# A hybrid DeltaNet and windowed-attention layer on one core: the first head's inverse gets its pool beside that head's tiles and stands ahead of the projections' close, and the ordering plan prices transfers by packets

## The chip, the cores and the metric

The kernel runs on one core of a Trainium2 chip. A core has five instruction streams: PE (TensorE, matrix products), DVE (VectorE), ACT (ScalarE), POOL (GpSimd) and SP (SyncE, which here issues every transfer); 16 DMA engines move the data between HBM and the on-chip memories SBUF and PSUM. Every stream runs its instructions in the order in which they were built. The metric is the device time of one execution in microseconds (us).

## The reference

One layer over 2048 positions of width 1024, all in float32. After a row norm, one projection feeds two groups of heads:

```python
h = rms_norm(x, norm_w[l])
proj = h @ w_in[l]
dn_q, dn_k, dn_v, dn_z, dn_beta, dn_decay, sw_q, sw_k, sw_v, sw_z = split(proj, cuts)
dn = gated_deltanet_bidir(dn_q, dn_k, dn_v, dn_beta, dn_decay, ...)
dn = rms_norm(dn, dn_out_norm_w[l]) * silu(dn_z)
sw = windowed_gqa_with_sinks(sw_q, sw_k, sw_v, ...) * silu(sw_z)
x = x + concatenate([dn, sw]) @ w_out[l]
```

The first group is a gated DeltaNet of 4 heads of 128, scanned forward and backward: a centred convolution of width 5 with SiLU on q, k and v, then for each chunk the inverse of a unit triangular matrix built from the keys, and a state that goes from chunk to chunk. The second is attention of 8 query heads of 64 over a window of 128 to each side, with two key heads, rotary positions and a sink for each head. Both are gated by SiLU of a projection, put together, and multiplied by the output weights.

## The kernel before

Matrix products that need float32 precision are made of three fp32r products: an operand is split into a high part (ACT copies it, rounded) and a low part (DVE subtracts). The chunks of the scan are 128 positions long, so each head has 16, walked from both ends.

Phase A (`phase_a`) holds half of the positions at a time, as `xhi` and `xlo`. For each half it projects keys, values and queries of the attention, then for its 8 chunks interleaves attention with the other projections: `conv_pair` (q, k, v of the DeltaNet, with their convolution) and `gate_pairs` (the gates). `gate_pairs` makes tiles `zo` of 128 x 2 x 512 (L211) out of products `pf_z`, applies a half-angle tanh on ACT (L213) and a product on DVE (L214), and stores them (L217). The gates of the second half are not run there; they are handed on as `late`.

Phase B (`phase_b`) works head by head:

- `pre_front(h)` loads keys, queries (`kq`, two buffers) and values (`vt`) of four chunks at a time in the order `FRONT`, and decays (`dc`). PE transposes them (`tr`, `trv`) and multiplies keys with keys and queries (`gh`); DVE makes `ma` of that, which is stored to HBM as `m_d`.
- `solve(h)` loads the small diagonal blocks back (`X`, `L`, 32 x 32 each, 128 of them at once), fills `X` on POOL and eliminates column by column with 62 small operations on DVE (L741, L745). It stores the result as `x_d` (L746).
- `invert(h)` takes four groups of chunks, one after the other. For each it loads `xc` from `x_d` twice (L757), transposes on DVE (L758), sums two parts of `ma` on POOL (`g`, L761), copies the blocks into zeroed tiles `iv` (L763 to L767), and runs five rounds of four products on PE (`pi`, L772) with ACT copies between (L781 to L796). The inverse lands in `ma`.
- `scan(h)` walks the 16 chunks in both directions: for each it loads `kqc` (L810, four buffers a direction) and runs the products `pk`, `py` and `po`, with ACT and DVE between. After chunk 12 and at the end `post` norms the sums, gates them with `zt` and stores `mix_dn`.
- `sw_units` multiplies the attention's half of the output projection, in 32 units: loads `mxs`, `xrs` and weights `woss`, twelve matmuls `pcs` (L600 to L602), a store `part`. They fill PE between the steps of the scans. After the last scan, `out_dn` adds the DeltaNet's half (`pcd`).

Buffers come from pools that lie as two stacks in SBUF, one from the left and one from the right, and a tile waits for the last users of whatever lay at its place. The projections' pools `xp`, `wp` and `bp` lie on the right and close with `wide.close()` after `late` and `solve(0)`. The tiles of `invert` (pool `qb`: `xc`, `xt`, `g`, `b1`, `iv`, and some of the keys and values of later heads) and of the scan are opened on the right after that close, so they lie where the projections' buffers were.

In what order the instructions stand on each engine is neither the program's order nor written out by hand. `set_order` builds the graph of dependences with estimated costs and plans it forwards and backwards several times as a list schedule; the best plan's order is then fixed for PE, DVE, ACT, POOL and SP. For a transfer the plan has an issue cost of 500 ns on SP (`cost`), a latency of 2400 ns (`LAG`) and a time on a shared bus (`move`), and transfers follow each other on the bus (`bus`). `plan` is the function that walks the graph.

## Time and profile before

| | us |
|---|---|
| device time, median of 3 runs | 1291.93 |
| lowest and highest of them | 1291.03, 1295.85 |
| the profiled execution | 1291.8 |
| its span in the trace | 1290.0 |
| PE busy in the span | 1231.0 |
| DVE busy | 903.9 |
| ACT busy | 718.4 |
| POOL busy | 509.8 |

The page gives for each engine its busy time and, for groups of instructions, the time that the engine stood idle just before them and what ended it. Busy shares are means over stages of different kinds: the projections and the attention up to about 784 us, the four heads with the first half of the output projection to about 1195 us, and the second half to the end. A row of the timeline has the start, the duration, the engine, the line of the program, the operation, what it writes and reads, and how many follow each other. An f32 product on PE leaves two records, an fp32r product and a transpose one.

### The profile page before, as it was taken

Reading aid. Unit: us, or ns where it says so; the run is one execution under the profiler, and the core shown is the slowest. Engines: PE = TensorE matmul, PEld = TensorE weight load, DVE = VectorE, ACT = ScalarE, POOL = GpSimd, SP = SyncE. Lnnn points to the kernel's source line nnn. Section 1 sums busy time; section 2 is a strip of 40 time slices with the busy share of each in tenths; the row PEclk is TensorE's granted clock in tenths of the full one; section 3 lists DMA queues with packets and bytes.
Section 4 is the critical chain, followed back from the end, with each engine's and each line's share of the span. In section 5 each row is a group of like instructions: output and inputs, shape, how many; then the busy total and the mean of one; then the engine's idle time right before and its main releaser. Section 6 shows DMA issues by size and latency. Waiting matters only on the chain.

```text
span 1290.0 us, 22619 instructions
## 1 busy us (share of the span) xinstructions
PE 1231.0 (95%) x7162; PEld 1058.8 (82%) x7162; DVE 903.9 (70%) x2266; ACT 718.4 (56%) x2121; POOL 509.8 (40%) x876
## 2 busy tenths in 40 slices
PE   6999989999999999999999997999799899999998
PEld 6998778888889998888888886788688689898876
DVE  4422388999975689999986474689579869656433
ACT  5422254776744577777664325768657845675310
POOL 2230053757612297665320104833582482640000
PEclk9999999999999999999999997999999999999999
DMA  7442243322544433422127736966965875644765
GB/s 260 148 131 84 84 163 121 116 83 90 156 149 145 127 104 103 150 90 75 71 93 234 219 100 204 254 176 200 282 162 174 267 204 172 196 152 133 253 236 207
DMA packets 225511, 205.36 MB, mean 159 GB/s; under 512 B 48496, under 2 KB 175088, under 8 KB 225392
## 3 DMA queue, kind: packets, MB, share of 16 engines
q1 hardware_dynamic: 225392, 203.92, 50.9%
q8 instruction: 57, 0.93, 0.3%
q14 instruction: 62, 0.51, 0.1%
HBM read 138.79 MB, written 65.08 MB: 158 GB/s over the span
## 4 chain that ended last, share of the span: by engine, by line
PE 68%; DVE 13%; issue 6%; DMA 6%; ACT 4%; POOL 3%; SPq 0%; DVEq 0%; POOLq 0%; ACTq 0%
PE pf_c L190 5%; PE pf_c L191 5%; PE pf_c L192 5%; PE pf_z L190 4%; PE pf_z L191 4%; PE pf_z L192 4%; PE pi L772 3%; PE pt L364 3%; DVE acc L241 2%; PE pq_q L201 2%; PE pq_q L202 2%; PE pq_q L203 2%; PE pcd L563 2%; PE pcd L564 2%; PE pcd L562 2%
## 5 line engine op out<-in xcount | busy, mean ns | idle before, releaser
L190 PE MATMUL pf_c<-xhi,wh_c 128*128 128x512 f32 x384 | 151.2, 406 | 3.2 <-DVE acc L241 3.2
L241 DVE SCALAR_TENSOR_TENSOR acc<-pf_c,cw,acc 128x512 f32<-128x512 f32 (+2 forms) x192 | 140.0, 742 | 17.0 <-ACT acc L237 16.1
L191 PE MATMUL pf_c<-xlo,wh_c 128*128 128x512 f32 x384 | 151.0, 404 | 0.0
L192 PE MATMUL pf_c<-xhi,wl_c 128*128 128x512 f32 x384 | 149.8, 404 | 0.0
L359 POOL TENSOR_SCALAR pr<-pr,st 128x384 f32<-128x384 f32 (+1 forms) x128 | 84.8, 679 | 73.2 <-DVE st L357 49.9
L192 PE MATMUL pf_z<-xhi,wl_z 128*128 128x512 f32 x256 | 90.8, 401 | 0.0
L191 PE MATMUL pf_z<-xlo,wh_z 128*128 128x512 f32 x256 | 90.8, 399 | 0.0
L190 PE MATMUL pf_z<-xhi,wh_z 128*128 128x512 f32 x256 | 89.8, 400 | 0.0
L190 PEld LDWEIGHTS pf_c<-xhi,wh_c 128*128 128x128 f32 x384 | 72.7, 190 | 16.9 <-DVE acc L241 3.6
L350 ACT ACTIVATE pr<-pr,st 128x384 f32<-128x384 f32 (+1 forms) x128 | 76.1, 596 | 16.4 <-DVE st L349 14.3
L191 PEld LDWEIGHTS pf_c<-xlo,wh_c 128*128 128x128 f32 x384 | 72.6, 190 | 13.7
L192 PEld LDWEIGHTS pf_c<-xhi,wl_c 128*128 128x128 f32 x384 | 72.4, 189 | 13.8
L368 ACT ACTIVATE ph<-pt 128x512 fp32r<-128x512 f32 x92 | 53.7, 594 | 46.9 <-PE pt L364 41.3
L345 DVE CUSTOM_DVE_ANT_0 pr<-s,mask,sink 128x384 f32<-128x384 f32 (+1 forms) x128 | 72.7, 592 | 4.8 <-PE pt L364 2.5
L364 PE MATMUL pt<-ident,pr 128*128 128x128 f32 x368 | 71.5, 275 | 1.5 <-POOL pr L359 1.4
L826 ACT ACTIVATE yk<-py,ck 128x128 f32<-128x128 f32 x120 | 43.8, 365 | 48.4 <-PE py L821 47.2
L684 POOL TENSOR_TENSOR nk<-ssk,pw 128x4 f32<-128x4 f32 x16 | 16.9, 1059 | 131.0 <-DVE ssk L683 95.0
L703 DVE SCALAR_TENSOR_TENSOR ma<-gh,bp,dc 128x256 f32<-128x256 f32 x128 | 55.0, 476 | 19.4 <-PE gh L694 15.2
L369 DVE TENSOR_TENSOR pl<-pt,ph 128x512 fp32r<-128x512 f32 x92 | 62.0, 683 | 6.9 <-ACT ph L368 6.6
L364 PEld LDWEIGHTS pt<-ident,pr 128*128 128x128 f32 x368 | 48.1, 140 | 16.8 <-POOL pr L359 4.1
L202 PE MATMUL pq_q<-wh_q,xlo 128*128 128x256 f32 x256 | 61.5, 283 | 0.0
L201 PE MATMUL pq_q<-wh_q,xhi 128*128 128x256 f32 x256 | 61.1, 285 | 0.0
(253 smaller groups left out, 3798.4 us busy)
## 6 DMA issues: line engine op xcount, KB each, us to landing
kqc<-kq_d SPq DMA_DIRECT2D x120, 128.0 KB, 2.9
ws_c<-wt SPq DMA_DIRECT2D x48, 256.0 KB, 3.4
xr<-x SPq DMA_DIRECT2D x16, 512.0 KB, 5.3
ws_z<-wt SPq DMA_DIRECT2D x32, 256.0 KB, 3.6
kq<-kq_d SPq DMA_DIRECT2D x16, 512.0 KB, 5.4
m_d<-ma SPq DMA_DIRECT2D x32, 256.0 KB, 5.2
mxs<-mix_sw SPq DMA_DIRECT2D x32, 256.0 KB, 3.6
xrs<-x SPq DMA_DIRECT2D x32, 256.0 KB, 3.5
```

The costliest lines, as they stand in the source:

```text
L190: T.matmul(ps, hi[:, k, cs], xhi[b][:, k], start=(k == 0), stop=False)
L191: T.matmul(ps, hi[:, k, cs], xlo[b][:, k], start=False, stop=False)
L192: T.matmul(ps, lo[:, k, cs], xhi[b][:, k], start=False, stop=(k == KC - 1))
L201: T.matmul(ps[:, :n], xh, hi[:, k, :n], start=(k == 0), stop=False)
L202: T.matmul(ps[:, :n], xl, hi[:, k, :n], start=False, stop=False)
L241: V.scalar_tensor_tensor(av, ps[:, lo:], cw[:, i, k : k + 1], av, ALU.mult, ALU.add)
L345: V.tensor_tensor_reduce(pr[j][:, :n], ps[:, :n], mask[:, lo * P : hi * P], 1.0, sink[:, hh : hh + 1], ALU.add, ALU.max, accum_out=mx[:, j ...
L350: A.activation(pr[j][:, :n], pr[j][:, :n], AF.Exp, bias=nm[:, j : j + 1], accum_out=den[:, j : j + 1])
L359: G.tensor_scalar(pr[j][:, :n], pr[j][:, :n], den[:, j : j + 1], 1.0, ALU.mult, ALU.mult)
L364: T.transpose(pt[:, j], pr[j][:, (kb - lo) * P : (kb - lo + 1) * P], ident)
L369: V.tensor_tensor(pl, ptf, ph.bitcast(F32), ALU.subtract)
L703: V.scalar_tensor_tensor(ma[d, c4][:, c], gh[:, k], bp[:, d, cc : cc + 1], gms[d][:, c : c + 1].to_broadcast([P, 2, P]), ALU.mult, ALU.mult,)
```

## The change

It has two parts. In the kernel, the pool `bp` closes with phase A instead of with the projections; the late gates write into a new pool `zp` of two buffers on the right, at the place that `bp` leaves. The inverse's pool `qb` is opened on the left, beside the first head's tiles (`hd0`, `q1`, `qa`), before the late gates. The six zeroed tiles and `invert(0)` stand in the program ahead of `wide.close()`. The keys and values of later heads that lay in `qb` get a pool of their own, `kx`, on the right.

In the plan, a transfer's time on the bus is no longer bytes at 300 bytes a ns. It counts pieces: the shorter contiguous run of the two sides, up to 2048 elements, at 8 ns and 0.148 ns an element each, over 16 engines. And after each transfer SP is free no sooner than 1000 ns before the bus is, which bounds the transfers that wait. Since the plan decides every order, instructions move on all engines and in all stages.

```diff
-        bp = wide.enter_context(tc.tile_pool(reuse_waits="tile", name="bp", bufs=5))
+        bp = ctx.enter_context(tc.tile_pool(reuse_waits="tile", name="bp", bufs=5))
...
-    def gate_pairs(todo, half, mid=None):
+    def gate_pairs(todo, half, mid=None, zp=bp):
...
-                o = bp.tile([P, 1030], F32, tag="big", name=f"zo{i}_{half}_{nb}")[:, :1024].rearrange("p (j s) -> p j s", j=2)
+                o = zp.tile([P, 1030], F32, tag="big", name=f"zo{i}_{half}_{nb}")[:, :1024].rearrange("p (j s) -> p j s", j=2)
...
     qa = pool("qa", stack=pre_stack)
+    qb = pool("qb", stack=pre_stack)
...
-        return (hd[p] if p < 2 else qb).tile([P, 4, P], F32, tag=f"{kind}{slot}", name=name, bufs=1)
+        return (hd[p] if p < 2 else kx).tile([P, 4, P], F32, tag=f"{kind}{slot}", name=name, bufs=1)
...
+    with tc.using_default_side("right"):
+        zp = pool("zp", 2, stack=wide)
     H = pre_front(0)
     for f in late:
-        f()
+        f(zp)
     solve(0, H)
+    zts = [[const(f"iv{j}_{i}", [P, 4, P], None, qb) for i in range(2 - j % 2)] for j in range(4)]
+    for grp in zts:
+        for a in grp:
+            G.memset(a, 0.0)
+    invert(0, H)
     wide.close()
     with tc.using_default_side("right"):
         rp = pool("rp", 2)
         hd.append(pool("hd1"))
         ps_s = pool("ps_s", space=PSUM)
-        qb = pool("qb", stack=pre_stack)
+        kx = pool("kx", stack=pre_stack)
         swp = pool("swp", SWW, stack=pre_stack)
-    zts = [[const(f"iv{j}_{i}", [P, 4, P], None, qb) for i in range(2 - j % 2)] for j in range(4)]
-    for grp in zts:
-        for a in grp:
-            G.memset(a, 0.0)
     fill = sw_units(swp)
-    invert(0, H)
...
+    def run(a):
+        inside = a.tensor.name in tiles and "DRAM" not in str(tiles[a.tensor.name].space)
+        r = 1
+        for step, c in reversed(list(a.ap)[1:] if inside else list(a.ap)):
+            if step != r:
+                break
+            r *= c
+        return min(r, 2048)
...
-            move[k] = a.ap[0][1] * size(a) * 4 / 300
+            count = a.ap[0][1] * size(a)
+            piece = min(run(x) for x in aps(insts[k][0].ins) + [a])
+            move[k] = count / piece * (8 + 0.148 * piece) / 16
...
                 bus = max(t, bus) + move[k]
+                free[e] = max(free[e], bus - 1000)
```

More of the change, by code (lines that the diff above doesn't have):

```diff
@@ L407, in phase_a @@
             consts = delta_setup(tc, t, ident, bd, gp, ap, bp, pj, q_pool)
-        sw = [lambda i=i: gate_pairs([(16 + i, [zsw_d[i], zsw_d[i + 1]])], half) for i in (0, 2)]
+        sw = [lambda zp=bp, i=i: gate_pairs([(16 + i, [zsw_d[i], zsw_d[i + 1]])], half, None, zp) for i in (0, 2)]
         conv = [lambda i=i: conv_pair(i, half) for i in (0, 4, 8, 2, 6, 10)]
@@ L411, in phase_a @@
             fill = conv
-            late = sw + [lambda i=i: gate_pairs([(12 + i, zdn_d[i : i + 2])], half) for i in (0, 2)]
+            late = sw + [lambda zp, i=i: gate_pairs([(12 + i, zdn_d[i : i + 2])], half, None, zp) for i in (0, 2)]
         else:
```

## The prediction

> **What bounds the kernel now.** I read the page first, then the busy time by stage, then the order of time around the stage that stands out.
>
> ```profile
> span 1290.0 us, 22619 instructions
> PE 1231.0 (95%) x7162; PEld 1058.8 (82%) x7162; DVE 903.9 (70%) x2266; ACT 718.4 (56%) x2121; POOL 509.8 (40%) x876
> PEclk9999999999999999999999997999999999999999
> ...
> 0.00:784.00 784.00, 764.77 (x4223) 653.54 (x4224) 567.70 (x1322) 431.89 (x1045) 306.94 (x472) 1.00 0.40 128
> 784.00:818.00 34.00, 25.44 (x123) 19.51 (x121) 19.73 (x47) 24.49 (x109) 21.66 (x42) 0.75 0.91 259
> 818.00:850.00 32.00, 29.76 (x198) 26.69 (x198) 17.98 (x46) 22.11 (x73) 26.45 (x59) 1.00 0.88 240
> 850.00:890.00 40.00, 39.84 (x290) 37.03 (x290) 38.04 (x125) 26.12 (x106) 7.16 (x9) 1.00 0.54 165
> 890.00:930.00 40.00, 30.81 (x180) 24.74 (x179) 31.35 (x95) 28.56 (x124) 19.30 (x28) 0.96 0.87 256
> 1000.00:1040.00 40.00, 33.97 (x196) 27.46 (x195) 29.84 (x91) 30.51 (x132) 20.81 (x42) 0.96 0.87 263
> ```
>
> PE is the bound nearly everywhere: 764.77 of 784 us in the projections, 39.84 of 40 at 850. The rows by stage are PE, PEld, DVE, ACT and POOL busy, then the granted clock, the DMA share and GB/s. One stage stands apart: 784 to 818, 123 matmul records in 34 us against 198 in the next 32, PE idle for 34 - 25.44 = 8.6 us, the clock 0.75, the one 7 in the page's clock row. It is the hole between the last gate projection and the first head's scan. What ends last in it shows in order of time (start, duration):
>
> ```profile
> 777.50 0.32 SPq L746 DMA_DIRECT2D x_d<-X  x1
> 780.00:782.00 2.00, 2.00 (x12) 1.69 (x11) 0.00 (x0) 0.90 (x4) 0.00 (x0) 1.00 0.00 0
> 783.46 0.60 PE L674 MATMUL tr<-ident,kq 128*128 128x128 f32 x4
> 791.46 0.43 SPq L757 DMA_DIRECT2D xc<-x_d  x1
> 792.54 0.53 SPq L654 DMA_DIRECT2D kq<-kq_d  x1
> ...
> 786.33 1.02 POOL L684 TENSOR_TENSOR nk<-ssk,pw 128x4 f32<-128x4 f32 x1 [35.37 <-DVE ssk L683]
> 787.32 1.26 POOL L761 TENSOR_TENSOR g<-ma 128x512 f32<-128x512 f32 x1
> 788.52 1.03 POOL L901 MEMSET iv<- 128x512 f32 x2
> 795.88 0.61 POOL L763 COPY iv<-xc 32x128 f32<-32x128 f32 x2
> 801.58 1.49 PE L772 MATMUL pi<-iv,g 128*128 128x128 f32 x6
> 816.48 0.49 PE L821 MATMUL py<-vs,ma 128*128 128x128 f32 x2
> 818.01 0.50 PE L600 MATMUL pcs<-wohs,mhs 128*128 128x512 f32 x1
> ```
>
> The small solve of head 0 stored its result x_d at 777.50, and nothing was on the DMA engines from 780 to 782: it had landed. Yet the inverse's loads of it (xc) are issued at 791.46, because its pool lay over the projections' buffers, and on SP they stood behind loads for the scan. Its first product comes at 801.58, the first scan product at 816.48, the first output-projection matmul at 818.01. From 783.46 PE has only the next head's front, whose loads take turns in two buffers.
>
> **The change, part by part.** *The moved inverse.* For head 0 it issues 8 loads on SP, 8 transposes on DVE, 6 fills and 84 sums and copies on POOL, 44 copies on ACT and 80 products on PE. In the changed program the fills and the first two sums stand on POOL ahead of the solve, where POOL waits 35.37 us (row at 786.33): they cost nothing there, and without that cover 6 x 0.52 + 2 x 1.26 = 5.6 us ahead of the first copy. On SP five xc stand directly behind x_d, then a load for the front, two for the scan, three gate stores and one more xc. On PE 44 inverse products instead of 24, and 20 scan products instead of 1, stand between the last gate matmul and the first output matmul; the 48 transposes and 14 gram products of the next front stay there. Their prices:
>
> ```profile
> 821.29 0.89 PE pi L772 x8
> 685.54 0.87 PE gh L694 x4
> 213.42 0.89 PE ptq L326 x8
> ```
>
> An f32 product leaves two records: 0.22 us for a product of 128 columns, 0.435 for a gram product of 256, 0.11 for a transpose. PE's real work between 783.46 and the first output matmul is now 48 x 0.11 + 14 x 0.435 + 25 x 0.22 = 16.9 us, in 34.55 us: 17.6 us are lost. Changed, it is 16.9 + 39 x 0.22 = 25.5 us. If that stretch lost nothing, the gain would be 17.6 us; if the first output matmul still came at 818.01, with 8.6 us more done ahead of it, 8.6 us. I take a stretch of 28.5 us, so 34.55 + 8.6 - 28.5 = 14.6 us, nearer the upper end: from the xc issue to the first scan product the old chain took 25.0 us, and started at 780 instead of 791.46 it gives at the latest 805, while the next front still needs two loads of kq in turn, which fill the stretch to about 812 (issue near 793 again, since 24 issues at about 0.5 us stand ahead of it on SP).
>
> The new wait is on SP: the xc loads hold the queue until x_d has landed. Behind them stand the loads for the front and the scan and three gate stores; for the stores wait the gates' two buffers, for the loads PE. The trace of x_d's transfers bounds the hold:
>
> ```profile
> DMA to landing us min/median/max: 1.9/4.2/6.8
> ...
> q1 hardware_dynamic: 26000, 16.65, 86.7%
> ...
> kq<-kq_d SPq DMA_DIRECT2D x4, 512.0 KB, 5.9
> mxs<-mix_sw SPq DMA_DIRECT2D x6, 256.0 KB, 4.4
> xrs<-x SPq DMA_DIRECT2D x5, 256.0 KB, 5.2
> part<-xrs SPq DMA_DIRECT2D x4, 256.0 KB, 3.4
> xc<-x_d SPq DMA_DIRECT2D x8, 64.0 KB, 5.3
> ```
>
> 1.9 to 6.8 us from 777.50 is 779.4 to 784.3; the empty DMA row puts it at 780, so it is over before the last gate's store is ready, and costs nothing up to about 783.
>
> The Trainium skill ("DMA: Bandwidth & Descriptors", "Two DMAs through the same engine are not ordered") speaks against this placing: a load of what another transfer wrote must wait for that one's completion before it is issued, so the wait sits on the queue. By it alone the sum loses up to the longest landing less the empty stretch, some 4 us; by the row at 780 nothing.
>
> *The clock.* The half-rate stretch belongs to the hole:
>
> ```profile
> 786.00:800.00 14.00, 8.72 (x28) 5.83 (x28) 7.37 (x20) 6.87 (x35) 7.45 (x15) 0.59 0.92 273
> ```
>
> 28 records in 14 us, at 0.59. It is inside the 17.6 us and is not counted twice. Changed, the same place has the inverse's first products as well. The Trainium skill ("TensorE: Matmul & The Clock Gate", "What's actually happening") has the clock fall to half after one idle window of about 3.4 us and rise after a busy one; the trace agrees with the fall. By it one window at half rate, if PE still starves once, would give back about 1.7 us.
>
> *What passes on.* The 14.6 us must live through 818 to 850, where the DMA share is 0.88 after 0.91. The DMA engines work 0.91 x 34 + 0.88 x 32 = 59.1 us of these 66: if every byte has to move first, only 6.9 us can be had by 850. But 15 of the transfers (mxs, xrs, part, 256 KB each, 3.8 of 16.65 MB) belong to the output projection, which fills PE later as well; at 850 to 890 the share is 0.54, and that holds them. After 850 PE and DVE are near full and pass a shift on. I take 12 us, nearer 14.6 than 6.9 for that reason.
>
> *The gates' ring.* The last gates write into 2 buffers instead of 5; eight tiles, six reuses.
>
> ```profile
> 728.78 5.51 SPq L217 DMA_DIRECT2D zsw_d<-zo  x3
> 742.70 0.59 SPq L732 DMA_DIRECT2D L<-m_d  x1
> 749.07 1.09 ACT L213 ACTIVATE zo<-pf_z 128x512 f32<-128x512 f32 x2 [1.71 <-PE pf_z L192]
> ```
>
> The tile that is written first at 749.07 needs the stores that were all issued by 734.3: zero. In the changed order one of them stands behind the solve's two loads, the second issued at 742.70; a store after it, with the 3.4 us of part above, still lands before 749. Below nothing is excluded, since no operation goes; above, a wait here costs PE only when it outlasts three PSUM banks.
>
> *The plan.* A transfer is now priced by packets, and SP may run only 1 us ahead of the engines. It reorders every queue a little. At the start the loads of the second block of x come up to 12 issues earlier, ahead of three waits on PE:
>
> ```profile
> 44.45 0.39 PE L201 MATMUL pq_kv<-wh_kv,xhi 128*128 128x272 f32 x1 [0.42 <-ACT sgq L260]
> 45.54 0.39 PE L202 MATMUL pq_kv<-wh_kv,xlo 128*128 128x272 f32 x1 [0.70 <-DVE xlo L167]
> 49.08 0.68 PE L201 MATMUL pq_kv<-wh_kv,xhi 128*128 128x272 f32 x3 [0.23 <-ACT xhi L166]
> ```
>
> That is 1.35 us at most. For head 2, x_d moves from 11 issues behind the next front's last kq load to 10 ahead of it, which can at best save the 6.0 us that PE idles at 1000 to 1040; for head 1 it moves two issues back, which can cost as much. Bounds -6 to +7; I take 1 us.
>
> **Sum.** 12 + 1 = 13 us off. The profiled execution took 1291.8 us (span 1290.0 and 1.8 around it), the median of the runs is 1291.93: 1291.8 - 13 = 1278.8, about 1279 us.
>
> **The rivals.**
> 1. *The burst is bound by DMA.* The share of 0.9 for 66 us speaks for it; the 0.54 after 850 and the hole's idle PE against it. Gain 4 to 6.9 us: 1285 to 1288.
> 2. *The later heads shrink too.* With the scan ahead, solve and inverse of heads 1 and 2 fall where DVE is free, and the idle 9.2 us at 890 and 6.0 at 1000 shrink by half: 13 + 7.6, so 1271.
> 3. *Slower: loads arrive too late for the output projection.* The plan keeps SP from running ahead, and assumes 2.4 us plus the packets, while mxs and xrs take 4.4 and 5.2 us in this stage. PE runs in a fixed order, so each of the 32 units can stop it at its first matmul. Now that is rare:
>
> ```profile
> L600 PE MATMUL pcs<-wohs,mhs 128*128 128x512 f32 x128 | 55.9, 437 | 4.2 <-DVE ma L703 1.5 <-ACT mhs L594 1.3 <-ACT vs L715 1.3
> 844.18 4.33 DMA mxs<-mix_sw
> ```
>
> 4.2 us in all between 818 and 1200, though such a load is on the chain at 844.18. At 0.7 us more for each unit it is 22.4 us: 1279 + 22.4 = 1301. It decides from 0.6 us a unit (19.5 us, the gain and 0.5%). Against it: in the changed SP order these loads stand within a unit of where they stood.
> 4. *The change doesn't do what it says:* the xc loads land behind other traffic and the front's kq stays the last to end, so scan and output start as before: 0 to 2 us, 1290.
>
> **How the numbers follow.** Forecast 0.55 (its own range 1272 to 1284), rival 1 0.18, rival 2 0.12, rival 3 0.12, rival 4 0.03. Half a per cent is 6.5 us, about what a measurement here tells from no change: faster means under 1285.5, slower over 1298.4. Faster: 0.55 + 0.12 + 0.03 of rival 1 = 0.70; within 0.18; slower 0.12. The range of 1268 to 1292 takes in rivals 1, 2 and 4 and leaves out rival 3.
>
> **What would show it.** Right: first xc issue near 780, first inverse product near 786, first scan product by 805, first output matmul near 812, a granted clock over 0.9 in the 30 us after the last gate. Wrong: an idle SP at the first xc beyond 783 with stores behind it; ACT waiting at zo for a store; waits before L600 well over 4.2 us; PE idle in the projections well over 784 - 764.77 = 19.2 us; or a hole that has merely moved to the first turn of the heads.

## The result, and the profile after

The changed kernel takes 1286.16 us in the median of 15 runs (1283.45 to 1291.07), the kernel before 1293.82 us in 15 runs on the same chip: a ratio of 0.9948, with a 95% interval of 0.9937 to 0.9958. It is faster by half a per cent; 13 us were forecast, and 7.7 came. The profiled execution has a span of 1284.2 us where the one before has 1290.0, 5.8 us less, and the account below is made between these two. (Every transfer in both traces runs between HBM and SBUF: what PE writes to PSUM is read there by ACT and DVE, not by a transfer.)

From the page of the changed kernel, the span, the busy row, the granted clock in 40 slices, and two of the groups of products (busy time, mean ns, idle time before them with what ended it):

```profile
span 1284.2 us, 22568 instructions
PE 1227.4 (96%) x7162; PEld 1056.0 (82%) x7162; DVE 901.8 (70%) x2266; ACT 718.8 (56%) x2121; POOL 507.8 (40%) x876
PEclk9999999999999999999999999999899999999999
...
L190 PE MATMUL pf_z<-xhi,wh_z 128*128 128x512 f32 x256 | 87.0, 403 | 0.5 <-DVE zo L214 0.5
...
L600 PE MATMUL pcs<-wohs,mhs 128*128 128x512 f32 x128 | 57.7, 451 | 5.0 <-ACT mhs L594 5.0
```

The 7 in the clock row, the hole of before, is gone. The same stages as before, of the changed kernel (start and end, length, busy time and records of PE, PEld, DVE, ACT and POOL, clock, DMA share, GB/s):

```profile
0.00:784.00 784.00, 764.99 (x4217) 651.95 (x4218) 568.70 (x1324) 431.75 (x1043) 320.25 (x499) 1.00 0.41 129
784.00:818.00 34.00, 28.30 (x197) 25.48 (x195) 21.27 (x55) 30.11 (x129) 26.26 (x60) 0.95 0.90 265
818.00:850.00 32.00, 28.77 (x177) 25.11 (x178) 20.58 (x56) 20.40 (x67) 11.78 (x19) 1.00 0.89 249
850.00:890.00 40.00, 39.12 (x278) 35.24 (x276) 38.27 (x124) 29.12 (x124) 8.31 (x7) 1.00 0.62 185
890.00:930.00 40.00, 33.18 (x185) 26.82 (x185) 23.41 (x74) 25.30 (x105) 21.48 (x46) 0.91 0.92 272
1000.00:1040.00 40.00, 35.72 (x234) 30.80 (x234) 28.07 (x85) 30.07 (x127) 28.49 (x68) 1.00 0.83 237
```

From 784 to 818 there are 197 records where there were 123, at a clock of 0.95 where it was 0.75. But PE is busy for only 28.3 of these 34 us; and 818 to 850 has 177 records where it had 198. Part of the new work ahead was paid back behind.

To count it without that shift, take a stretch that ends with the same work in both: from the last gate product to the end of the first quarter of the output products `pcs`, then on to the first product of the second output half. Of the kernel before:

```profile
783.62:877.29 93.67, 82.87 (x512) 71.61 (x511) 64.33 (x176) 61.49 (x230) 52.52 (x107) 0.91 0.78 222
877.29:1194.89 317.60, 293.64 (x2043) 261.88 (x2041) 237.12 (x710) 209.34 (x805) 148.70 (x297) 0.99 0.65 195
```

and of the changed kernel:

```profile
784.48:870.30 85.82, 76.89 (x510) 68.75 (x509) 61.41 (x172) 61.30 (x231) 38.75 (x78) 0.98 0.82 238
870.30:1186.75 316.45, 293.16 (x2029) 260.65 (x2028) 236.25 (x706) 209.43 (x804) 146.78 (x297) 0.98 0.66 195
```

The first row of each holds almost the same work, 512 and 510 records, in 93.67 and 85.82 us: the hole gave 7.9 us. PE's busy time fell by 6.0 us for the same records, which is the clock (0.91 to 0.98), and its idle time only from 10.8 to 8.9 us. So between these two executions three quarters of the gain is the clock.

The order of time in the changed kernel around the last gate product (784.48):

```profile
770.61 0.32 SPq L747 DMA_DIRECT2D x_d<-X  x1
775.32 6.51 SPq L758 DMA_DIRECT2D xc<-x_d  x5
784.75 1.06 PE L773 MATMUL pi<-iv,g 128*128 128x128 f32 x8
...
794.33 0.65 SPq L655 DMA_DIRECT2D kq<-kq_d  x1
795.93 0.39 PE L822 MATMUL py<-vs,ma 128*128 128x128 f32 x2
798.78 0.49 PE L831 MATMUL po<-yk,ks 128*128 128x128 f32 x2 [2.24 <-ACT yk L827]
801.12 1.12 PE L675 MATMUL tr<-ident,kq 128*128 128x128 f32 x4 [1.63 <-DMA kq<-kq_d]
...
806.34 0.52 SPq L655 DMA_DIRECT2D kq<-kq_d  x1
811.41 0.66 PE L675 MATMUL tr<-ident,kq 128*128 128x128 f32 x4
818.84 1.13 ACT L716 ACTIVATE vs<-trv,nk 128x128 f32<-128x128 f32 x4
820.02 0.50 PE L600 MATMUL pcs<-wohs,mhs 128*128 128x512 f32 x1
```

and of the kernel before, the same load, transposes and scalings:

```profile
804.80 0.53 SPq L654 DMA_DIRECT2D kq<-kq_d  x1
812.17 0.60 PE L674 MATMUL tr<-ident,kq 128*128 128x128 f32 x4
816.84 1.12 ACT L715 ACTIVATE vs<-trv,nk 128x128 f32<-128x128 f32 x4
```

The inverse starts 16.8 us earlier than before (784.75 against 801.58) and the scan 20.6 us earlier (795.93 against 816.48), both as forecast or better. The first output product does not: 820.02 us, 35.5 us after the last gate product, where it was 34.4 before. It depends on the next head's front, not on the inverse: its PSUM tile (`bank(0)`) takes the one buffer `tr` of the pool `ps_t`, which holds the front's last value transposes `trv` until ACT's scalings `vs` have read them. The four `vs` end at 819.97 us and the output product starts 0.05 us later; before, 817.96 and again 0.05. So the moved inverse took 9.0 us off the time behind the first output product (from there to the quarter, 59.3 us before and 50.3 now) and nothing off the time ahead of it.

What PE waits for from 784 to 870, by engine and line (us in total, times, the longest):

```profile
PE po L831 <- ACT yk L827: 2.9, 2, 2.2
PE pcs L600 <- ACT mhs L594: 2.4, 2, 1.7
PE tr L675 <- DMA kq<-kq_d: 1.6, 1, 1.6
PE pi L773 <- ACT ma L791: 0.8, 1, 0.8
PE tr L675 <- ACT vs L716: 0.5, 1, 0.5
PE pk L813 <- DVE r L815: 0.5, 1, 0.5
```

6.6 of the 8.7 us listed are waits for ACT: it now makes the inverse's copies, the scan's, and the next front's squares and scalings in one stretch, 30.11 of 34 us busy where it had 24.49. The chain that ended last passes from the inverse to a load in four steps (start, duration):

```profile
791.86 1.28 POOL g L762
...
793.86 0.30 POOL ma L785
794.16 0.07 SPq L758
...
794.33 6.75 DMA kq<-kq_d
```

POOL's copy gives a buffer back, an `xc` load that had waited for it on SP goes out, and behind it the next front's `kq`, which takes 6.75 us to land. From 804.88 to 818.55 the same chain stays on ACT, in the front's squares, scalings and decays and the copies between them, with gaps of at most 0.2 us.

### The profile page after: what moved, and what is told of

It is laid out like the page before. It is cut to its first block, busy times and chain, and to the rows that moved or that the text cites. A ratio compares the mean times of both kernels' runs of the same rounds, so it can differ in the third digit from the quotient of the medians.

```text
span 1284.2 us, 22568 instructions
## 1 busy us (share of the span) xinstructions
PE 1227.4 (96%) x7162; PEld 1056.0 (82%) x7162; DVE 901.8 (70%) x2266; ACT 718.8 (56%) x2121; POOL 507.8 (40%) x876
## 4 chain that ended last, share of the span: by engine, by line
PE 67%; DVE 9%; DMA 9%; ACT 5%; POOL 4%; issue 4%; SPq 1%; DVEq 0%; POOLq 0%; ACTq 0%
PE pf_c L190 5%; PE pf_c L191 5%; PE pf_c L192 5%; PE pf_z L190 4%; PE pf_z L191 4%; PE pf_z L192 4%; PE pi L773 3%; PE pt L364 3%; PE pcd L562 2%; PE pcd L563 2%; PE pcd L564 2%; DVE acc L241 2%; PE pcs L601 2%; PE py L822 1%; PE pcs L600 1%
## 5 line engine op out<-in xcount | busy, mean ns | idle before, releaser
L241 DVE SCALAR_TENSOR_TENSOR acc<-pf_c,cw,acc 128x512 f32<-128x512 f32 (+1 forms) x192 | 140.4, 742 | 10.4 <-ACT acc L237 8.1
L359 POOL TENSOR_SCALAR pr<-pr,st 128x384 f32<-128x384 f32 (+1 forms) x128 | 88.8, 711 | 72.3 <-DVE st L357 56.5
L190 PE MATMUL pf_z<-xhi,wh_z 128*128 128x512 f32 x256 | 87.0, 403 | 0.5 <-DVE zo L214 0.5
L191 PE MATMUL pf_z<-xlo,wh_z 128*128 128x512 f32 x256 | 86.5, 399 | 0.0
L192 PE MATMUL pf_z<-xhi,wl_z 128*128 128x512 f32 x256 | 85.3, 398 | 0.0
L600 PE MATMUL pcs<-wohs,mhs 128*128 128x512 f32 x128 | 57.7, 451 | 5.0 <-ACT mhs L594 5.0
```

Of the source, the lines that this page charges most:

```text
L190: T.matmul(ps, hi[:, k, cs], xhi[b][:, k], start=(k == 0), stop=False)
L191: T.matmul(ps, hi[:, k, cs], xlo[b][:, k], start=False, stop=False)
L192: T.matmul(ps, lo[:, k, cs], xhi[b][:, k], start=False, stop=(k == KC - 1))
L241: V.scalar_tensor_tensor(av, ps[:, lo:], cw[:, i, k : k + 1], av, ALU.mult, ALU.add)
L359: G.tensor_scalar(pr[j][:, :n], pr[j][:, :n], den[:, j : j + 1], 1.0, ALU.mult, ALU.mult)
L600: T.matmul(ps, mh[:, k], wh[:, k], start=(k == 0), stop=False)
```

## The experiments

Every run is compared with runs of the kernel before on the same chip. All the stages together, from the trace of each run (us): A, from the start to the last key and value product `pq_kv`; B, on to the last gate product; I, from there to the first inverse product `pi`; C, from the last gate product to a quarter of `pcs`; D, from there to the last product.

| | ratio and interval | A | B | I | C | D |
|---|---|---|---|---|---|---|
| before | 1 | 424.7 | 358.9 | 18.0 | 93.7 | 409.1 |
| changed | 0.9948 (0.9937 to 0.9958) | 420.9 | 363.6 | 0.3 | 85.8 | 410.3 |
| e1_pool_old_plan | 0.9982 (0.9965 to 0.9998) | 425.6 | 364.0 | 0.3 | 84.0 | 410.5 |
| e2_plan_only | 1.0055 (1.0035 to 1.0075) | 421.4 | 362.3 | 13.4 | 93.0 | 420.6 |
| e3_no_bound | 0.9969 (0.9954 to 0.9984) | 427.7 | 364.3 | 1.1 | 88.4 | 407.7 |
| e4_old_price | 0.9930 (0.9905 to 0.9955) | 419.4 | 365.7 | 0.3 | 85.0 | 409.1 |
| e5_kq3 | 1.0000 (0.9983 to 1.0017) | 421.5 | 360.2 | 28.3 | 98.5 | 409.0 |
| e6_kqc2 | 0.9946 (0.9924 to 0.9968) | 422.1 | 365.3 | 0.3 | 87.2 | 407.3 |
| e7_zp3 | 1.0131 (1.0107 to 1.0155) | 424.7 | 368.1 | 33.2 | 101.8 | 413.7 |
| e8_bound_only | 0.9992 (0.9980 to 1.0004) | 419.1 | 358.5 | 29.4 | 92.8 | 414.3 |
| e10_half_kqc | 0.9923 (0.9905 to 0.9942) | 424.0 | 363.4 | 0.3 | 83.3 | 410.0 |
| e11_vs_dve | 0.9987 (0.9969 to 1.0006) | 422.2 | 360.4 | 0.3 | 85.2 | 413.4 |
| e12_vs_twice | 1.0012 (0.9992 to 1.0033) | 423.7 | 366.5 | 4.7 | 89.7 | 412.0 |
| e13_xc6 | 0.9974 (0.9956 to 0.9993) | 423.0 | 363.0 | 0.3 | 85.2 | 417.1 |
| e14_both | 0.9896 (0.9859 to 0.9934) | 424.3 | 364.4 | 0.3 | 84.4 | 406.4 |
| e15_bound500 | 0.9867 (0.9841 to 0.9893) | 415.4 | 362.5 | 0.3 | 85.3 | 408.0 |
| e16_bound2000 | 0.9926 (0.9898 to 0.9954) | 422.3 | 368.9 | 0.3 | 84.1 | 403.7 |
| e17_old_price_vs | 0.9921 (0.9887 to 0.9954) | 420.2 | 364.7 | 0.3 | 83.4 | 411.8 |
| e18_bound250 | 0.9930 (0.9904 to 0.9955) | 421.1 | 367.0 | 1.1 | 87.5 | 406.9 |
| e19_before_bound500 | 0.9963 (0.9945 to 0.9981) | 416.5 | 360.8 | 22.6 | 96.9 | 412.6 |

Any edit makes the plan anew, for all engines and all stages. The changed kernel and e6, e7, e10, e11, e12 and e13 have the same rule for the plan, and differ only in buffers or work behind stage A: their A spreads over 4 us (420.9 to 424.7) and their D more widely. A difference of 2 us in one stage of one run therefore proves nothing. The stages come from one profiled execution, the ratios from all: the profiled executions of e1, e8 and e11 were the fastest of their ten (of e11 6.5 us below its median), that of e13 was 2 us above its median, and e3's was the slowest of its ten, 2.4 us above.

### The parts of the change, each without the others

e1 has the moved pools and the plan of before. Edit, against the changed kernel:

```diff
-            count = a.ap[0][1] * size(a)
-            piece = min(run(x) for x in aps(insts[k][0].ins) + [a])
-            move[k] = count / piece * (8 + 0.148 * piece) / 16
+            move[k] = a.ap[0][1] * size(a) * 4 / 300
...
-                free[e] = max(free[e], bus - 1000)
```

> The changed kernel with the old plan (a transfer at 300 bytes a ns, no bound on those waiting). Theory A (the inverse's move is worth some 7 us in the stretch between the last gate and the first output matmul, the new plan nets about nothing because it gains 4 to 5 us in the first half of the projections and loses as much in the second): 1286 to 1288 us, ratio to before about 0.995, the first scan product some 15 to 20 us ahead of before, the last gate matmul within 1 us of before's 783.6. Theory B (the plan makes the gain, the move only shifts the hole to the heads): 1292 to 1295, ratio 0.999 to 1.001.

e2 is the kernel before with these lines of the changed plan put in, price and bound:

> The kernel before with the new plan alone (packets and bound), inverse and pools as before. Theory A: 1291 to 1295, ratio about 0.999, with the last conv matmul of the first half some 4 us earlier than before's 318.3 mark and that lead gone by the last gate; the hole as wide as before (34 us). Theory B: 1286 to 1288.

e3 is the changed kernel without its bound (the last line above alone), e4 the changed kernel with the old price and the bound.

> The changed kernel without the line that bounds the transfers waiting; packets are counted. Theory A, with the bound as what moves transfers: within 2 us of the run with the old plan (1286 to 1288), and neither the lead of 4 us in the first half nor its loss in the second. Theory B: 1290 to 1294.

> The changed kernel with the bound but bytes at 300 a ns in place of packets. Packets change the price of most transfers little (0.43 us either way for the scan's loads, 0.41 instead of 0.22 for the inverse's), so theory A expects what the changed kernel takes, 1285 to 1288, and the stage times like it. Theory B with packets as the cause: 1290 to 1294.

The window from the last gate product to a quarter of `pcs`, of e1:

```profile
789.59:873.62 84.03, 78.11 (x536) 70.32 (x535) 59.01 (x164) 63.94 (x247) 40.38 (x77) 1.00 0.84 242
```

and the same window and the next of e2, to the first product of the second output half:

```profile
783.73:876.74 93.01, 82.00 (x496) 71.59 (x495) 63.44 (x174) 60.59 (x227) 52.80 (x106) 0.89 0.79 223
876.74:1205.63 328.89, 297.86 (x2055) 264.07 (x2053) 238.75 (x712) 210.93 (x807) 146.68 (x297) 0.98 0.65 187
```

Theory B, that the plan makes the gain, has fallen: e2 is slower than the kernel before, at 1303.28 us outside both of its ranges. But e1 is not where theory A had it either: 1293.54 us lies in theory B's range, and its last gate product came at 789.59 us, 6 us behind 783.6. The hole belongs to the moved pools: 84.0 us with them alone at a clock of 1.00, 93.0 us with the plan alone at 0.89. Yet e1 as a whole gains only 0.2%: its stage B is 5.1 us longer than before. And the plan, which alone loses 0.55%, takes another 3.8 us off the span (1288.0 to 1284.2) where the pools are moved. Put in alone, it loses in the heads: 328.9 us in e2's second row against 317.6, with 31.0 us in which PE is not busy in place of 24.0. The two parts do not add up: alone 0.2% gained and 0.55% lost, together 0.5% gained. Of the plan the bound is the useful half: e4 differs from e1 by the bound alone, and their intervals lie apart (0.9930 against 0.9982). Without the bound (e3, 1291.53 us, theory B's range) A is 427.7 us and the ratio 0.9969; with the old price under the bound (e4, 1286.46 us, as theory A had it) nothing is lost.

What stage B pays shows in e4, from the last convolution product to the last gate product. This is all that PE waited for there:

```profile
PE pf_z L190 <- DVE acc L241: 3.8, 1, 3.8
```

The first gate product stops for DVE's convolution once. e1 has the same wait with 3.0 us, the changed kernel a wait of 0.5 us for DVE's `zo` (page, above); before, PE has none there.

e8 is the kernel before with the bound alone, at 1000 ns, e19 the same at 500 ns:

```diff
                 bus = max(t, bus) + move[k]
+                free[e] = max(free[e], bus - 1000)
```

> The kernel before with the bound alone: SP is free no sooner than 1000 ns before the bus, transfers priced by bytes as before, the pools as before. With the packet price as well the projections gained 3 us (to 421.4) and the later heads lost 11 (the last head's output-projection half began at 1205.6 in place of 1194.9). If the packet price makes that loss, the bound alone ends at 1288 to 1291. If the bound makes it with the old place of the pools, it ends at 1298 to 1304 like the two together. If it is a matter of the single plan, anything between.

> The kernel before, pools as they were, with the bound alone at 500 ns. The first stage does not know of the moved pools, so it ends at 415 to 417. If the later heads lose as with 1000 ns (5 us) and the hole stays at 93 us, the ratio is 0.994 to 0.998: then the moved pools are worth 8 to 13 us once the bound is there, against 2 us without it. If the bound alone does it all, 0.987 to 0.990.

e8 came out between its two forecasts, e19 as expected but for the hole, 96.9 us instead of 93. Both shorten A (419.1 and 416.5 us), and both give most of it back after the last gate product, in C or D, where the pools are the old ones. From the last gate product to the end (C and D), the four kernels with the old pools take 502.8 to 513.6 us; the changed kernel, e1, e3 and e4 494.0 to 496.1. With the bound at 500 ns the moved pools are worth the step from 0.9963 to 0.9867 (e15, below), 1.0%; without any bound, 0.2%.

### What sets the rest of the hole

e5 gives the next front's `kq` three buffers, and makes room with `kqc` of two buffers and `jk` of one; e6 has the `kqc` of two alone; e7 gives the gates three buffers, and makes room with `jk` of one.

```diff
-            kq = q1.tile([P, 2, 512], F32, tag="kq", name=f"kq{h}_{c4}", bufs=2)
+            kq = q1.tile([P, 2, 512], F32, tag="kq", name=f"kq{h}_{c4}", bufs=3)
...
-                    jk = q1.tile([P, P], F32, tag="jk", name=f"jk{h}_{c4}_{j}_{c}", bufs=3)
+                    jk = q1.tile([P, P], F32, tag="jk", name=f"jk{h}_{c4}_{j}_{c}", bufs=1)
...
-                    kqc = rp.tile([P, 2, P], F32, tag=f"kqc{d}", name=f"kqc{nm}", bufs=4)
+                    kqc = rp.tile([P, 2, P], F32, tag=f"kqc{d}", name=f"kqc{nm}", bufs=2)
...
-        zp = pool("zp", 2, stack=wide)
+        zp = pool("zp", 3, stack=wide)
```

> The changed kernel with three buffers in place of two for the front's key-and-query tile kq, paid for by two scan tiles kqc of each direction fewer and one scratch tile jk in place of three. Theory F: the 35.5 us from the last gate product (784.5) to the first output product (820.0) hold 25.5 us of work and lose 10 because the next head's fronts go in step with their two kq buffers (issues at 794.3, then only 806.3 when the first gram products have freed one). Then the third kq is issued before 800, the first output product comes 3 to 6 us sooner after the last gate product (30 to 33 us), and the time is 1280 to 1284. Theory D (the DMA engines are full there, 0.90 of 784 to 818 and 0.89 of 818 to 850): the same bytes in another order, the stretch stays at 34 to 37 us, the time at 1285 to 1289.

> The changed kernel with two buffers in place of four for the scan's tile kqc in each direction: at most 4 of these 128 KB loads wait ahead of the scan in place of 8, so 0.5 MB fewer lie in the burst after the last gate (9.65 MB were moved from 784 to 820). Theory D (the DMA engines and the queue that issues to them bound the burst): the first output product comes 2 to 4 us sooner, about 32 us after the last gate product, and the time is 1282 to 1285 unless later scan steps wait for their kqc, which would show as waits of the products pk for DMA kqc. Theory F (the two kq buffers set it): stretch 34 to 37 us, time 1285 to 1289. It is also the control for the run with three kq buffers, which has these two kqc.

> The changed kernel with three gate buffers zp in place of two, one scratch tile jk in place of three. My step that the ring of two costs nothing: the stage from the last convolution product to the last gate product stays at 102 us (102.31 with two, 101.06 before with five), the time at 1284 to 1288. Rival: the ring costs the 1 to 3 us by which this stage is longer with the moved pools (102.3 to 104.3 against 101.1); then it is 101 us or under and the time 1283 to 1285.

e5 and e7 missed both expectations, for a reason I had not seen: with one `jk` the first head's front, and with it the small solve, come later. In e7:

```profile
807.08 0.78 SPq L747 DMA_DIRECT2D x_d<-X  x1
826.03 1.18 PE L773 MATMUL pi<-iv,g 128*128 128x128 f32 x8
```

`x_d` is stored at 807.08 where the changed kernel has 770.61, and the first inverse product comes 33.2 us after the last gate product. So their times say nothing of `kq` or of the gates' ring; in e5 the front's next two loads of `kq` still go out 10.1 and 20.6 us after the last gate product (9.8 and 21.9 in the changed kernel). But they measure something better, what the hole costs by the delay of the inverse (columns I and C): 0.3 to 1.1 us late, C is 83.3 to 88.4; 4.7 late, 89.7; 13 to 29 late, 92.8 to 98.5; 33.2 late, 101.8. The hole's length goes with the delay of the inverse, over 18 us of C. So the moved pools help only as long as the solve has ended by the last gate product, and in the changed plan it has: `x_d` goes out 6.9 us earlier than before. e6 leaves C at 87.2 and the time at 1287.46, as theory F had it for this run: the scan's early loads are not what holds the hole.

What the delay of the inverse does not change is the first output product. In all 20 kernels it comes 32.0 to 39.1 us after the last gate product, 35.1 us in e8, where the inverse starts 29.4 us late. In 18 of them it starts 0.05 or 0.06 us after the last `vs` of the next head's front, in e10 0.16 and in e6 1.9 us after it.

e10 halves the bytes of the scan's loads and leaves out their query half, e11 takes ACT's scalings of the second head's front to DVE, e12 doubles them on ACT, e13 gives the inverse's loads six buffers, e14 has the edits of e10 and e11 together.

```diff
-                    kqc = rp.tile([P, 2, P], F32, tag=f"kqc{d}", name=f"kqc{nm}", bufs=4)
-                    dma(kqc, kq_d[h][:, :, sc])
+                    kqc = rp.tile([P, 1, P], F32, tag=f"kqc{d}", name=f"kqc{nm}", bufs=4)
+                    dma(kqc, kq_d[h][:, 0:1, sc])
...
-                    T.matmul(po[:, 2], kqc[:, 1], st[d], start=True, stop=True)
+                    T.matmul(po[:, 2], kqc[:, 0], st[d], start=True, stop=True)
```

```diff
-                A.activation(vs[c4][:, c], tr[:, c], AF.Copy, scale=nk[:, cc : cc + 1])
+                if h == 1:
+                    V.tensor_scalar(vs[c4][:, c], tr[:, c], nk[:, cc : cc + 1], None, ALU.mult)
+                else:
+                    A.activation(vs[c4][:, c], tr[:, c], AF.Copy, scale=nk[:, cc : cc + 1])
```

```diff
-                A.activation(vs[c4][:, c], tr[:, c], AF.Copy, scale=nk[:, cc : cc + 1])
+                for _ in range(1 + (h == 1)):
+                    A.activation(vs[c4][:, c], tr[:, c], AF.Copy, scale=nk[:, cc : cc + 1])
```

```diff
-                xc = qb.tile([P, 4, 32], F32, tag="xc", name=f"xc{h}_{d}_{c4}", bufs=4)
+                xc = qb.tile([P, 4, 32], F32, tag="xc", name=f"xc{h}_{d}_{c4}", bufs=6)
```

> The changed kernel with the scan's tile kqc cut to its key half: 64 KB a step in place of 128, the same products, and the query half is left out (the key half stands in for it). It takes 0.64 MB of the 9.65 MB out of 784 to 820 and half of the scan's loads from each head. Theory D (bytes bound the burst, 268 GB/s): 0.64 MB is 2.4 us, the first output product comes 2 to 3 us sooner after the last gate product, and 2 to 4 us more are gained by a quarter of the output products; time 1280 to 1283. Theory F: the stretch stays at 34 to 37 us and the time at 1284 to 1288.

> The changed kernel with the 16 scalings of the values vs of the second head's front on DVE in place of ACT: 16 x 0.29 = 4.7 us of work leave ACT in the stretch after the last gate product, where ACT is busy 31.6 of 35.5 us and DVE 22.1. Theory A (ACT bounds the stretch; I had counted the work of PE alone): from the last gate product to the first output product 31 to 33 us in place of 35.5, to a quarter of the output products 82 to 84 in place of 85.8, and the time 1282 to 1284. Theory D (the DMA engines, 0.92 busy there, bound it): 35 to 37 us, 85 to 87, and 1285 to 1288.

> The changed kernel with the same 16 scalings made twice on ACT, the second over the first: 4.7 us more of ACT work in the stretch, no bytes and nothing else. Theory A: the stretch grows by 3 to 5 us, to 39 to 41 us up to the first output product or to 89 to 91 up to a quarter of them, and the time is 1289 to 1291. Theory D: 35 to 37 us, 85 to 87, and the time 1285 to 1288, since ACT has 4 us free there.

> The changed kernel with six buffers in place of four for the inverse's loads xc: the fifth of them held the transfer queue for 3.8 us (775.3 to 781.8) until POOL had copied the first one, and behind it stood the next front's loads, the last of which before the stop is issued at 794.33 and lands after 6.75 us. Theory G (this hold on SP is what the wait of the moved loads costs): the next front's first load is 3 us earlier, the stretch 32 to 33 us, the time 1282 to 1284. Theory A (ACT): the loads are earlier, ACT's 31.6 us stay, the stretch 34.5 to 36, the time 1285 to 1288.

> The changed kernel with both: the scan's tile kqc cut to its key half (the query half left out, the key half used for it) and the second head's 16 scalings of vs on DVE. Apart they made the hole, from the last gate product to a quarter of the output products, 83.3 and 85.2 us long in place of 85.8, with 7.2 and 8.9 us of idle PE in place of 8.9. Theory AD (ACT and the DMA engines bind side by side): together more than the sum, the hole 79 to 81.5 us with under 6 us idle, the time 1280 to 1283 against a kernel before of 1294. Theory L (neither is the bound; the next front's own chain from load over transposes, squares and products is, whatever its engines' load): 82.5 to 85 us, 7 to 9 us idle, time 1283 to 1288.

The rows of e11, from the last gate product to the first output product and on to the quarter:

```profile
782.61:816.19 33.58, 26.66 (x192) 23.26 (x191) 25.16 (x69) 27.11 (x116) 25.42 (x53) 1.00 0.92 274
816.19:867.80 51.61, 49.61 (x324) 44.40 (x323) 40.63 (x121) 30.06 (x100) 16.64 (x34) 1.00 0.76 222
```

and of e12:

```profile
790.19:828.40 38.21, 28.21 (x167) 23.55 (x165) 23.70 (x63) 34.21 (x144) 29.27 (x70) 0.91 0.97 266
828.40:879.84 51.44, 50.28 (x338) 45.37 (x338) 40.67 (x119) 30.43 (x105) 16.55 (x29) 1.00 0.73 206
```

More work on ACT lengthens C by 3.8 us, as expected, though this plan also starts the inverse 4.5 us later. Less work on ACT gives 0.6 us where 2 to 4 were expected (and e11's whole gain is within its interval of none), so ACT alone does not set it. As whole kernels the two opposite edits both came out slower than the changed kernel (ratios 0.9987 and 1.0012), and their 1293.17 and 1296.12 us lie outside every range named for them: only the stage, not the time, bears on ACT. Fewer bytes bring the first output product 3.6 us nearer to the last gate product, but only 2.5 us are left at the quarter, and the time of 1284.51 is outside what theory D named (it is in theory F's range, whose stretch the run missed). Both together, of e14:

```profile
788.74:873.16 84.42, 76.45 (x515) 69.08 (x513) 62.01 (x182) 57.62 (x220) 41.81 (x85) 0.98 0.77 224
```

84.42 us with 8.0 us idle and 1284.11 us in all, within what was expected if neither binds. The theory that ACT and the DMA engines bind side by side has fallen. e13 spares SP the hold and gets 33.8 us to the first output product, 85.2 to the quarter, and loses 6.8 us in D: theory G missed, and 1291.94 us is outside theory A's range too. With the hold gone the next front's `kq` still goes out 9.2 us after the last gate product, so the hold did not delay it. So no single load or hold among these edits sets the remaining idle time. What is left is the front's own chain from load over transposes, squares and products, as theory L had it, and the first output product has to wait for its end. The traces show two forms of that chain. In the changed kernel it runs over one load and then ACT, as above. In e11, with the 16 scalings off ACT, it runs over the two loads in turn, with PE's work behind each:

```profile
792.85 6.06 DMA kq<-kq_d
803.25 6.20 DMA kq<-kq_d
```

That fits how little relieving ACT gave. What shortens the chain, and what an output tile with a PSUM buffer of its own would give, is not tested.

### The bound of the plan

e15, e16 and e18 are e4 with another bound, e17 is e4 with the scalings on DVE as in e11.

```diff
-                free[e] = max(free[e], bus - 1000)
+                free[e] = max(free[e], bus - 500)
```

> The changed kernel with the old price of bytes and the bound at 500 ns in place of 1000. With 1000 and the old price the projections' last key and value product ended at 419.4 (424.7 before) and the ratio was 0.993. If a nearer bound keeps loads off the queue ahead of waits still better, the projections end at 418 to 420 again and the ratio is 0.990 to 0.994. If the bound's size is a matter of chance in the plan, the stages move by 2 to 4 us either way, and the ratio lies from 0.992 to 1.000.

> The changed kernel with the old price of bytes and the bound at 2000 ns. Without any bound the first stage took 425.6 to 427.7 us, with 1000 ns 419.4 to 420.9. If the bound's nearness matters, 2000 ns lies between, 421 to 425, and the ratio is 0.994 to 0.998. If any bound of this order does it, 419 to 421.5 and 0.991 to 0.995.

> The changed kernel with the old price of bytes, the bound at 1000 ns, and the second head's 16 scalings of vs on DVE: the best run so far (ratio 0.993) with 4.7 us of work taken from ACT in the hole. By theory A the hole shrinks from 85.0 to 82 to 84 and the ratio is 0.990 to 0.992; by what the same move gave in the changed kernel (85.8 to 85.2, and 4 us lost in the later heads) the ratio is 0.993 to 0.998.

> The changed kernel with the old price of bytes and the bound at 250 ns. If the first stage goes on shrinking as the bound comes nearer, its last key and value product ends at 411 to 415 (415.4 at 500 ns) and the ratio is 0.983 to 0.987. If 500 ns was at the bottom (a load issued that late then holds PE), 415 to 420 and 0.987 to 0.993.

e15 came out better than either of its ranges and is the best of all kernels here: 1278.24 us in 4 runs (1276.5 to 1280.51) against 1294.47 before, 1.3% less. Its interval (0.9841 to 0.9893) lies clear of the changed kernel's. Its hole is no better:

```profile
777.84:863.17 85.33, 77.12 (x512) 68.61 (x511) 59.72 (x171) 60.53 (x231) 40.52 (x80) 0.98 0.84 241
```

Its gain is in A, 415.4 us, and e19 has the same bound with the old pools and 416.5. With the old price, A goes from 425.6 (no bound, e1) to 422.3 (2000 ns), 419.4 and 419.1 (1000 ns) and 415.4 and 416.5 (500 ns), and then back to 421.1 at 250 ns, where e18 missed both of its ranges for A (its ratio of 0.9930 is at the edge of the second). The whole way from no bound to 500 ns, 8 to 10 us, is clear of the 4 us by which A spreads under one rule; the single steps are not (with 1000 ns, e17 has 420.2), and that 500 is better than 250 rests on one plan at 250. e16's A is as expected if the nearness of the bound matters; its ratio is better than that for its D of 403.7, which no theory foresaw. e17's hole is 83.4 us, 1.5 less than e4's, as theory A had it, and e17 gives it back in D: its 0.9921 is no different from e4.

## Why the prediction was right or wrong

*The hole and its mechanism.* Right. First `xc` issue at 775.32 (forecast about 780), first inverse product 784.75 (786), scan 795.93 (by 805), and a clock of 0.95 from 784 to 818. The early `xc` is helped by a term that I did not forecast: `x_d` itself went out 6.9 us earlier than before, where I had kept its old time. The hold of SP by the first `xc` was real, 4.3 us for `x_d` to land (4.7 from its issue; my bounds of 1.9 and 6.8 were those of all transfers of `x_d`, the loads among them), and cost nothing seen: PE's only wait for the gates' tiles in the page is 0.5 us. The Trainium skill ("DMA: Bandwidth & Descriptors", "Two DMAs through the same engine are not ordered") has the issuing engine wait for the first transfer's completion before it issues a load of what that one writes; this hold is that wait. The loss of some 4 us that I had put beside it was not seen.

*The stretch of 28.5 us.* This is the step that failed. I added up PE's work ahead of the first output product, 25.5 us, and let only 3 us more be lost, because the products standing there would fill PE's idle time. From the last gate product to the first output product it took 35.5 us (784.48 to 820.02), and over the longer window that holds the same work the hole gave 7.9 us, not 14.6, under my lower bound of 8.6. The path was wrong: I ended the stretch near 812, with the next front's two loads of `kq`, and put at nothing what the front does behind them. The second of those loads went out at 806.34 and its transposes began at 811.41, about as forecast; from there the front's squares, products and scalings took 8.6 us more, and only then was the PSUM buffer free for the first output product. Before, it was 5.8 us from the transposes at 812.17 to the output product, and 34.4 us for the whole stretch: this path was there before the change, and the change did not touch it. The other term of the sum was right: 8.6 us of work moved ahead of the first output product, and behind it the traces give 9.0 us. With the measured stretches my own sum reads 34.4 + 8.6 - 35.5 = 7.5 us, close to the 7.9.

What came back of the 17.6 lost us was the clock, 6.0 us of busy time. By the rows from 784 to 818, taking the lower rate as half (0.50 in the 2 us rows from 790 to 804 before), 0.05 x 34 x 2 = 3.4 us at half rate are left of 0.25 x 34 x 2 = 17. The rule of windows (the Trainium skill, "TensorE: Matmul & The Clock Gate", "What's actually happening") agrees: 3.4 us is one of its windows. The idle time moved by 1.9 us only. PE's order is fixed, and products put there wait for ACT themselves, by the list above 2.9 us in the scan and 0.8 in the inverse. How the gain splits into clock and idle time differs from plan to plan, though: e1, with the same moved pools, idles 5.9 us in its 84.0 at a clock of 1.00, and e8, with the old pools, idles 16.0 us in its 92.8 at 0.94. I had read the 8.6 us of idle PE as a gap to be filled, and did not add up ACT, 30.11 us in that stretch and more than the whole of my 28.5. Relieving ACT alone does not bring the 28.5 either: e11 needs 33.6 us.

*What passes on.* Right as a share, as far as one trace each can show it: 12 of 14.6 was taken, 82%; of 7.9 us at the quarter 6.6 are left at the end (D is 1.2 us longer), 84%. The first rival's times, 1285 to 1288, hold the measured 1286.16. Its reason is borne out only in part: with 0.64 MB cut (e10) the first output product came 3.6 us sooner, but C gave only 2.5 us and 7.2 us of idle time stayed.

*The gates' ring, costed at zero.* The wait for the two buffers was as good as zero, 0.5 us. But stage B as a whole is 4.7 us longer in the changed kernel and 5.1 in e1, the pools alone, and no term of the sum stood for that. In e1 3.0 us of it are the first gate product waiting for DVE; the rest is not settled, nor whether it is the place of the pools or the single plan: over all the runs, B is 358.5 to 362.3 us with the old pools and 360.2 to 368.9 with the moved ones.

*The plan, 1 us.* Undersized, with the sign right beside the moved pools (alone, e2, the plan loses 0.55%): 3.8 us of the span from e1 to the changed kernel, inside the bounds of -6 to +7. I had looked for it in the order of two transfers in the heads; it came in the projections, stage A, 4.7 us from e1 to the changed kernel.

*The sum.* Forecast 12 + 1. Measured, in the same places: 7.9 in the hole, 1.2 lost after it, 4.7 lost in stage B, 3.9 gained in stage A: 5.9, which is the 5.8 us of the spans.

*Rivals 2, 3 and 4.* The later heads did not shrink: from 890 to 930 PE idles 6.8 us where it idled 9.2, but at a clock of 0.91, and D as a whole grew. Rival 3 did not come: the waits before L600 are 5.0 us in all, 4.2 before. Rival 4, which I gave 0.03, came true in one half: the front stayed the last to end, and the first output product came as before, 35.5 us after the last gate product (34.4 before). Its other half did not: the scan started 20.6 us earlier.

## What to carry to other kernels

Before forecasting that a product will come sooner, follow what that product itself waits for, its output buffer included: here the first output product hung on the next head's front, which the change did not touch. When a hole is to be filled with work that has producers on other engines, add up every engine's work in the new stretch, not only that of the idle one. And split what is lost into idle time and clock. In a kernel whose order is planned, test each part alone and together: these two parts gained 0.5% only as a pair. So it is with how far the transfer queue may run ahead: 500 ns was worth 0.4% with the old pools (e19) and 1.2% on top of the moved ones (e1 to e15).

## What the runs showed of the hardware

How little less idling can bring the clock back: before, 10.8 us of idle time in the hole's window went with a clock of 0.91 over 93.67 us; the changed kernel idles 8.9 us with nearly the same records, at 0.98, and is busy 6.0 us less. e11, with the same 8.9 us (85.19 less 76.27 by its two rows), had a clock of 1.00 in both of its rows. So the total does not decide it. The half-rate stretches last 3.41 us in the changed kernel and 17.07 us, five times that, before. The one in the changed kernel follows 3.41 us in which PE was busy for 0.72 us, in pieces:

```profile
797.35:800.76 3.41, 0.72 (x4) 0.53 (x4) 1.56 (x4) 2.81 (x9) 3.02 (x10) 1.00 1.06 331
800.76:804.18 3.42, 3.06 (x15) 3.06 (x16) 1.44 (x4) 1.90 (x10) 0.70 (x2) 0.50 0.76 157
```

So the clock fell without a single wait of 3.4 us; the longest in the hole was 2.24 us. And e11 has a stretch almost as empty, and kept its clock:

```profile
795.65:799.06 3.41, 0.76 (x6) 0.41 (x4) 3.18 (x6) 2.91 (x7) 3.20 (x5) 1.00 0.97 290
```

The clock gained in such an exchange is therefore not something that these runs let one forecast from idle time alone.
